# The start of a hybrid encoder on one core: parameter loads on ScalarE's queue, RMS roots on GpSimd, x tile 3 in halves, and other fill-in steps among the mLSTM heads

## The chip, the cores and the metric

The kernel runs on one core of a Trainium2 chip. The metric is the device time of one execution in microseconds; three executions of the kernel before gave 1367.3 to 1371.68, with a median of 1370.09. The engines are TensorE (PE), VectorE (DVE), ScalarE (ACT), GpSimd (POOL) and SyncE (SP), which only issues DMAs here.

## What is computed

One layer of an encoder on x of 512 tokens by 1024 channels, in float32. Cut to what matters:

```python
h = rms_norm(x, norm_mix_g[l])
z = jnp.einsum('bsd,dc->bsc', h, w_in[l])
y_a = jnp.einsum('bsw,wd->bsd', mlstm_branch(z, ...), w_up_a[l])           # 4 heads, both directions
y_b = jnp.einsum('bsw,wd->bsd', diff_attention_branch(z, ...), w_up_b[l])  # 4 heads, ALiBi
g_a = jax.nn.sigmoid(z[..., OFF_GATE:OFF_GATE + D_MODEL])
g_b = jax.nn.sigmoid(z[..., OFF_GATE + D_MODEL:])
x = x + jnp.einsum('bsd,de->bse', g_a * y_a + g_b * y_b, w_out[l])
h2 = rms_norm(x, norm_ffn_g[l])
x = x + expert_choice_ffn(h2, ...)    # 16 experts, 64 tokens each, 1024 -> 2048 -> 1024
return rms_norm(x, norm_f_g)
```

`rms_norm` divides each row of x by the root of its mean square and multiplies by a gain per channel.

## The kernel before

**The trunk** (everything up to the router) works on transposed activations. At the start four tiles of x (`xt`, 128 tokens by 1024 channels) are loaded, squared and summed on ScalarE (L266), turned into reciprocal roots two tiles at a time (`rsqrt_act`: small VectorE steps and a ScalarE square root), and scaled into `xs`. TensorE transposes `xs` into eight PSUM tiles `hps` (L280), first seven of the eight channel blocks of every tile, then the last. ScalarE and VectorE evacuate each of the eight as a high part `hH` and a rest `hL` (`split_evac`, L233 and L234), scaled by the gains in `pc`. The column tile `pc` is the transpose of `prow`, 69 rows of small parameters that six DMAs bring in.

Every projection then takes three matmuls for each block of channels (`zT`: L310 to L312), of weight blocks `raw` that are split likewise into `sp`: the copy on ScalarE (L249), the subtraction on VectorE (L250); for the first block, `pre[0]`, the copy is L283 and the subtraction L284 on GpSimd. `raw` has five buffers. The gate weights `graw`, the gate biases `bi` and `bf`, `lamt` and the router's `wr` come in beside them.

**Order of the work.** Up to `start_order.close()` VectorE and ScalarE run their instructions in the order in which the code is written, and TensorE does so through the whole trunk. GpSimd's and SyncE's instructions are put in order by the framework's scheduler when the kernel is built; on the chip each engine takes its own instructions strictly in the built order. Each DMA that SyncE or ScalarE issues counts on one of eight semaphores, `DMAHW0` to `DMAHW7`, taken in turn, and an issue waits until the last DMA on its semaphore has landed. Each engine's instructions are held up by what waits ahead of them.

**Among the mLSTM heads** TensorE's order is a list of steps. `mlstm_head(h)` yields after each of four score blocks (`sc`, L569 to L571, whose weights VectorE makes at L582), after the first two value products (`pn`, L591) and at the end; VectorE reads `pn` at L599 and so gives its two PSUM buffers back. Between them stand fill-in steps `more`: for heads 0 and 1 the q and k projections of head h + 2, four steps of 12 matmuls; for heads 2 and 3 steps of `gate_b`, the gated up-projection of the attention branch (two half projections, then one step through `w_up_b`).

**The feed-forward part** streams 16 experts' weights through a ring of eleven 2 MB buffers (`mw`), which lie where tiles of the trunk lay. SyncE issues the loads (L995 for gate and up weights, L1163 for down weights) in the order in which they are used.

Of the kernel before, what the change touches and what calls it, by code (L numbers as in the profile page):

```python
# [71 lines left out]
def kernel(  # L72
# [60 lines left out]
    def rsqrt_act(dst, ssq, scale, pool):  # L133
        w = pool.tile([P, 3, 4], F32, tag="rsq", name="rsq", bufs=4)
        v, u = w[:, 0, 0:dst.shape[-1]], w[:, 1, 0:dst.shape[-1]]
        ve.tensor_scalar(v, ssq, scale, EPS, op0=OP.mult, op1=OP.add)
        se.activation(u, v, AF.Sqrt)
        ve.reciprocal(dst, u)
        ve.tensor_mul(u, dst, dst)
        ve.tensor_mul(u, u, v)  # L140
        ve.tensor_scalar(u, u, -0.5, 1.5, op0=OP.mult, op1=OP.add)
        ve.tensor_mul(dst, dst, u)

# [52 lines left out]
    first_sqrt = consts.tile([P, 1], F32, name="first_sqrt")  # L196
    se.activation(first_sqrt, ident[:, 0:1], AF.Sqrt)
# [1 line left out]
    sy.dma_start(prow[0:8], norm_mix_g[0].rearrange("(k p) -> k p", p=P))
    sy.dma_start(prow[8:16], norm_ffn_g[0].rearrange("(k p) -> k p", p=P))  # L200
    sy.dma_start(prow[16:24], conv_b[0].rearrange("(k p) -> k p", p=P))
    sy.dma_start(prow[24:64], conv_w[0].rearrange("w (k p) -> (w k) p", p=P))
    sy.dma_start(prow[64:68], mlstm_norm_g[0].rearrange("(k p) -> k p", p=P))
# [1123 lines left out]
```

## Time and profile before

| | |
|---|---|
| median of 3 executions | 1370.09 us (1367.3 to 1371.68) |
| profiled execution | 1370.63 us, of which its span 1368.3 us |
| busy in the span | PE 95%, DVE 30%, ACT 22%, POOL 10% |
| data moved | 444.02 MB, 325 GB/s over the span |
| first projection matmul (L310) | 16.70 us |
| mLSTM heads | from about 195 to 285 us |
| first weight load of the experts | 390.25 us |

Times inside the profile count from the span's start; the execution's time is longer than the span by what lies before its first and behind its last instruction. The share of busy time is a mean over stages that have different limits: start, trunk, router and expert weights are to be read apart.

### The profile page before, as it was taken

To read this page: it belongs to the slowest core of one execution; us is meant where nothing else is said; L and a number is where in the kernel's file an instruction comes from. 1 tells how busy PE (TensorE), PEld (TensorE's weight loads), DVE (VectorE), ACT (ScalarE), POOL (GpSimd) and SP (SyncE) were. 2 spreads that over 40 slices of the span, in tenths; PEclk is the share of its full clock that TensorE was granted. 3 is DMA by queue.
4 is the path that set the end of the run, shared out by engine and by line. 5 is a ranking of instruction groups with operands and counts; after the bars stand their busy time and mean duration, and the time that the engine had idled before them with its cause. 6 is when DMAs were issued, how large, how long until landed. Compare 5 with 4: busy or idle time off the path is not lost.

```text
span 1368.3 us, 16140 instructions
## 1 busy us (share of the span) xinstructions
PE 1301.3 (95%) x6566; PEld 711.8 (52%) x6566; DVE 415.5 (30%) x982; ACT 304.5 (22%) x621; POOL 131.1 (10%) x239
## 2 busy tenths in 40 slices
PE   8999999999999999999999998999899899889997
PEld 8988897888888534433433432423333242333332
DVE  5687759853443211020030020111102012010241
ACT  7676646433331010100000001000010000001030
POOL 3010212200111011000000000000000000000020
PEclk9999999999999999999999999999999999999999
DMA  7223242223478899999999999999999999999996
GB/s 205 64 64 89 81 109 62 63 77 107 134 280 344 339 425 427 427 428 427 429 428 427 428 427 428 427 428 428 428 427 429 428 427 427 427 428 427 428 427 276
DMA packets 81737, 444.02 MB, mean 325 GB/s; under 512 B 6353, under 2 KB 49431, under 8 KB 54656
## 3 DMA queue, kind: packets, MB, share of 16 engines
q1 hardware_dynamic: 79312, 438.43, 78.6%
q10 hardware_dynamic: 2240, 4.25, 1.3%
q8 instruction: 51, 0.84, 0.2%
q0 software_dynamic: 112, 0.33, 0.1%
q14 instruction: 22, 0.18, 0.0%
HBM read 440.58 MB, written 2.38 MB: 324 GB/s over the span
## 4 chain that ended last, share of the span: by engine, by line
PE 69%; DMA 22%; DVE 4%; issue 3%; ACT 2%; POOL 0%; POOLq 0%; SPq 0%; ACTq 0%; DVEq 0%
DMA w<-in_w_up_e_dram 21%; PE pgate L1083 14%; PE pup L1083 12%; PE pd L1167 7%; PE pg L1034 4%; PE zps L310 4%; PE zps L312 4%; PE zps L311 4%; PE pg L1151 3%; PE pt L1129 1%; PE bank L784 1%; PE bank L786 1%; PE bank L785 1%; PE pa L1053 1%; PE zps L352 1%
## 5 line engine op out<-in xcount | busy, mean ns | idle before, releaser
L1083 PE MATMUL pup<-w,xe 128*64 128x512 f32 x1024 | 240.1, 600 | 27.1 <-DMA w<-in_w_up_e_dram 27.1
L1083 PE MATMUL pgate<-w,xe 128*64 128x512 f32 x1016 | 243.7, 603 | 0.7 <-ACT sh L1272 0.7
L1167 PE MATMUL pd<-w,sh 128*64 128x512 f32 x1024 | 228.5, 597 | 15.4 <-DMA w<-in_w_down_e_dram 13.6
L1167 PEld LDWEIGHTS pd<-w,sh 128*64 128x64 f32 x1024 | 71.2, 137 | 162.6 <-issue 130.8
L1083 PEld LDWEIGHTS pup<-w,xe 128*64 128x64 f32 x1024 | 69.1, 136 | 165.4 <-issue 115.9
L1083 PEld LDWEIGHTS pgate<-w,xe 128*64 128x64 f32 x1016 | 63.0, 136 | 98.5 <-issue 85.2
L1146 DVE SCALAR_TENSOR_TENSOR mats<-pd,ga,mats 64x512 fp32r<-64x512 f32 x30 | 22.5, 750 | 289.1 <-ACT mats L1144 288.6
L310 PE MATMUL zps<-hH,sp 128*128 128x512 f32 x256 | 101.9, 398 | 0.8 <-DVE hL L234 0.8
L312 PE MATMUL zps<-hH,sp 128*128 128x512 f32 x256 | 100.0, 391 | 0.0
L311 PE MATMUL zps<-hL,sp 128*128 128x512 f32 x256 | 99.9, 390 | 0.0
L250 DVE TENSOR_TENSOR sp<-raw,sp 128x512 fp32r<-128x512 f32 x114 | 78.1, 688 | 54.6 <-ACT sp L249 52.0
L1034 PEld LDWEIGHTS pg<-ohr,xn 128*128 128x128 f32 x512 | 64.8, 196 | 45.4 <-issue 44.6
L249 ACT ACTIVATE sp<-raw 128x512 fp32r<-128x512 f32 x114 | 70.9, 630 | 69.5 <-PE zps L620 27.6
L1034 PE MATMUL pg<-ohr,xn 128*128 128x128 f32 x512 | 75.8, 293 | 0.2 <-DVE ohr L1027 0.2
L1284 DVE TENSOR_TENSOR sh<-sh,pup 128x512 f32<-128x512 f32 x32 | 20.6, 684 | 140.2 <-PE pup L1083 133.3
L1144 ACT ACTIVATE mats<-pd,ga 64x512 fp32r<-64x512 f32 x30 | 20.5, 683 | 191.6 <-PE pd L1167 191.3
L1038 ACT ACTIVATE xe<-pg,gff 128x128 f32<-128x128 f32 x32 | 11.8, 368 | 228.8 <-PE pg L1034 228.8
L1133 ACT ACTIVATE sh<-pt 128x512 f32<-128x512 f32 x16 | 9.6, 598 | 237.6 <-PE pt L1129 237.6
L1047 POOL TENSOR_SCALAR mats<-iota,slot 128x64 fp32r<-128x64 f32 x64 | 26.8, 444 | 313.4 <-PE pt L1064 288.2
L310 PEld LDWEIGHTS zps<-hH,sp 128*128 128x128 f32 x256 | 48.1, 188 | 10.6 <-POOL sp L284 1.0
L312 PEld LDWEIGHTS zps<-hH,sp 128*128 128x128 f32 x256 | 48.1, 188 | 10.4
L311 PEld LDWEIGHTS zps<-hL,sp 128*128 128x128 f32 x256 | 48.1, 188 | 9.5
(337 smaller groups left out, 1551.8 us busy)
## 6 DMA issues: line engine op xcount, KB each, us to landing
w<-in_w_down_e_dram SPq DMA_DIRECT2D x59, 2048.0 KB
w<-in_w_gate_e_dram SPq DMA_DIRECT2D x56, 2048.0 KB
w<-in_w_up_e_dram SPq DMA_DIRECT2D x56, 2048.0 KB
raw<-in_w_in_dram SPq DMA_DIRECT2D x44, 512.0 KB
w<-in_w_up_e_dram SPq DMA_DIRECT2D x16, 1024.0 KB
w<-in_w_gate_e_dram SPq DMA_DIRECT2D x15, 1024.0 KB
w<-in_w_down_e_dram SPq DMA_DIRECT2D x8, 1024.0 KB
raw<-in_w_out_dram SPq DMA_DIRECT2D x8, 512.0 KB
```

Source lines behind the costliest of these rows:

```text
L249: se.activation(sp[:, 0], raw, AF.Copy)
L250: ve.tensor_sub(sp[:, 1], raw, sp[:, 0].bitcast(F32))
L310: pe.matmul(zp, w[:, 1], hT(hH, k), start=(k == 0), stop=False)
L311: pe.matmul(zp, w[:, 0], hT(hL, k), start=False, stop=False)
L312: pe.matmul(zp, w[:, 0], hT(hH, k), start=False, stop=(k == ND - 1))
L1034: pe.matmul(pg, xn[t][:, c0:c0 + 255:2], ohr[:, t], start=(t == 0), stop=(t == NT - 1))
L1047: (gp if j else ve).tensor_scalar(oa[:, t, j * CAP:(j + 1) * CAP], iota, slot[:, t, e:e + 1], None, op0=OP.is_equal)
L1083: pe.matmul(pu[s * 64:(s + 1) * 64, c], xe[:, b, half:half + CAP], wt[:, c0:c0 + 512], start=(b == 0), stop=(b == ND - 1))
L1146: ve.scalar_tensor_tensor(yb[r, 1, c], src[r], ga[r, e % 2], yb[r, 0, c].bitcast(F32), op0=OP.mult, op1=OP.subtract)
L1151: pe.matmul(pq, oaT[:, v, t], yb[:, i, cols], start=(i == 0), stop=(i == 1))
L1167: pe.matmul(pd[s * 64:(s + 1) * 64], hid_col(q, i), wt[:, i * D + h * 512:i * D + (h + 1) * 512], start=(c == 0), stop=(c == 15))
L1284: ve.tensor_mul(sg[:, cols], sg[:, cols], pu[:, i])
```

## The change

It has two places.

1. At the start. The six loads into `prow` are issued by ScalarE instead of SyncE, and SyncE issues the first two weight blocks `pre` directly behind x, ahead of `graw`. The first activation function is Exp instead of Sqrt. The roots are taken on GpSimd by a power of -0.5 (`rms`), for tiles 0 and 1 together, tile 2 and tile 3. Tile 3 is squared in two halves, one on ScalarE and one on VectorE, and scaled in two halves. The copies of `pre[0]` on ScalarE now stand ahead of the scaling of tile 3, and the parameters' transpose ahead of x's.
2. Among the heads. For heads 0 and 1 `gate_b` is appended to the list of fill-in steps, and every head gives 2, 2, 1 and 1 steps to its four slots instead of 2, 1, 1 and 2.

```diff
-    first_sqrt = consts.tile([P, 1], F32, name="first_sqrt")
-    se.activation(first_sqrt, ident[:, 0:1], AF.Sqrt)
+    first_exp = consts.tile([P, 1], F32, name="first_exp")
+    se.activation(first_exp, ident[:, 0:1], AF.Exp)
     prow = gt("prow", (NROW, P))
-    sy.dma_start(prow[0:8], norm_mix_g[0].rearrange("(k p) -> k p", p=P))
...
-    sy.dma_start(prow[68:69], diff_norm_g[0:1])
+    se.dma_start(prow[0:8], norm_mix_g[0].rearrange("(k p) -> k p", p=P))
...
+    se.dma_start(prow[68:69], diff_norm_g[0:1])
+    pre = [load_head(c) for c in (DQ, DK)]
     graw = gt("graw", (P, ND, NGATE))
     sy.dma_start(graw, wi[:, MG:MG + NGATE].rearrange("(k p) c -> p k c", p=P))
-    pre = [load_head(c) for c in (DQ, DK)]
...
-    ss = r4.tile([P, 2, NT], F32, name="ss")
-    xs = []
-    for t in range(NT):
...
-        se.activation(xs[t], xt[t], AF.Square, accum_out=ss[:, 0, t:t + 1])
-        if t % 2 == 1:
-            rsqrt_act(ss[:, 1, t - 1:t + 1], ss[:, 0, t - 1:t + 1], 1.0 / D, consts)
-            for i in (t - 1, t):
-                if i == 2:
-                    se.activation(xs[i], xt[i], AF.Copy, scale=ss[:, 1, i:i + 1])
-                else:
-                    ve.tensor_scalar(xs[i], xt[i], ss[:, 1, i:i + 1], None, op0=OP.mult)
+    ss = r4.tile([P, 4, NT], F32, name="ss")
+    gp.memset(ss[:, 3], -0.5)
+
+    def rms(t0, t1):
+
+        v = ss[:, 0, t0:t1]
+        gp.tensor_scalar(v, v, 1.0 / D, EPS, op0=OP.mult, op1=OP.add)
+        gp.tensor_tensor(ss[:, 1, t0:t1], v, ss[:, 3, t0:t1], op=OP.pow)
...
+    for t in range(2):
+        se.activation(xs[t], xt[t], AF.Square, accum_out=ss[:, 0, t:t + 1])
+    rms(0, 2)
+    se.activation(xs[2], xt[2], AF.Square, accum_out=ss[:, 0, 2:3])
+    rms(2, 3)
+    for t in range(2):
+        ve.tensor_scalar(xs[t], xt[t], ss[:, 1, t:t + 1], None, op0=OP.mult)
+        x_T(t, range(ND - 1))
+
+    se.activation(xs[3][:, 0:512], xt[3][:, 0:512], AF.Square, accum_out=ss[:, 0, 3:4])
+    ve.tensor_tensor_reduce(xs[3][:, 512:], xt[3][:, 512:], xt[3][:, 512:], 1.0, 0.0, op0=OP.mult, op1=OP.add,
+                            accum_out=ss[:, 2, 3:4])
+    gp.tensor_add(ss[:, 0, 3:4], ss[:, 0, 3:4], ss[:, 2, 3:4])
+    rms(3, 4)
     sq = [sp_tile((4, P)) for _ in range(2)]
     for i in range(2):
         se.activation(sq[i][:, 0], pre[0][:, 4 * i:4 * i + 4], AF.Copy)
         last_sub = gp.tensor_sub(sq[i][:, 1], pre[0][:, 4 * i:4 * i + 4], sq[i][:, 0].bitcast(F32))
     pre[0] = sq
+    ve.tensor_scalar(xs[2], xt[2], ss[:, 1, 2:3], None, op0=OP.mult)
+    x_T(2, range(ND - 1))
+    ve.tensor_scalar(xs[3][:, 0:512], xt[3][:, 0:512], ss[:, 1, 3:4], None, op0=OP.mult)
+    se.activation(xs[3][:, 512:], xt[3][:, 512:], AF.Copy, scale=ss[:, 1, 3:4])
+    x_T(3, range(ND - 1))
...
-        more = steps(lambda: mlstm_q(h + 2), lambda: mlstm_k(h + 2)) if h < 2 else gate_b
-        for i, (n, m) in enumerate(((2, 2), (2, 1), (1, 1), (1, 2))):
+        more = [gate_b] if h > 1 else [steps(lambda: mlstm_q(h + 2), lambda: mlstm_k(h + 2)), gate_b]
+        for i, (n, m) in enumerate(((2, 2), (2, 2), (1, 1), (1, 1))):
             run(head, n)
             if (h, i) == (0, 1):
                 attn_out(3)
-            run(more, m)
+            for _ in range(m):
+                while next(more[0], 0) == 0:
+                    more.pop(0)
```

How the built programs stand against each other is shown at three places. The names in brackets are the semaphores that an instruction waits for. First ScalarE, at the start of the program. Before, behind the first activation (x tiles 0 to 3 are `x_63`, `x_65`, `x_67` and `x_69`; `raw` is the first weight block):

```order
L266 ACTIVATE xs,ss<-x_63 128x1024 [waits DMAHW1_49]
L266 ACTIVATE xs,ss<-x_65 128x1024 [waits DMAHW2_49]
L137 ACTIVATE rsq<-rsq 128x2 [waits DVE_49]
L266 ACTIVATE xs,ss<-x_67 128x1024 [waits DMAHW3_49]
L266 ACTIVATE xs,ss<-x_69 128x1024 [waits DMAHW4_49]
L137 ACTIVATE rsq<-rsq 128x2 [waits DVE_49]
L271 ACTIVATE xs<-x_67,ss 128x1024 [waits DVE_49,Activation_49]
L283 ACTIVATE sp<-raw 128x512 [waits DMAHW4_49]
L283 ACTIVATE sp<-raw 128x512
```

And now, at the same place:

```order
L188 DMA prow<-in_norm_mix_g_dram 8x128
L189 DMA prow<-in_norm_ffn_g_dram 8x128 [waits DMAHW0_49]
L190 DMA prow<-in_conv_b_dram 8x128 [waits DMAHW2_49]
L191 DMA prow<-in_conv_w_dram 40x128 [waits DMAHW4_49]
L192 DMA prow<-in_mlstm_norm_g_dram 4x128 [waits DMAHW6_49]
L193 DMA prow<-in_diff_norm_g_dram 1x128 [waits DMAHW0_49]
L270 ACTIVATE xs,ss<-x_63 128x1024 [waits DMAHW1_49]
L270 ACTIVATE xs,ss<-x_65 128x1024
L272 ACTIVATE xs,ss<-x_67 128x1024 [waits DMAHW3_49]
L278 ACTIVATE xs,ss<-x_69 128x512
L285 ACTIVATE sp<-raw 128x512 [waits DMAHW5_49]
L285 ACTIVATE sp<-raw 128x512
```

The six loads stand ahead of the Squares, with waits of their own: semaphore 0 is that of `gff` and then of the second `prow` load, semaphores 2 and 4 are those of x tiles 1 and 3, and semaphore 6 is that of the second weight block. The next row of ScalarE is the half scaling of tile 3 (L291, which waits for VectorE and GpSimd), and the eight evacuations stand behind it.

Second GpSimd, behind the memsets at the start of the program. Before:

```order
L284 TENSOR_TENSOR sp<-raw,sp 128x512 [waits DMAHW4_49,Activation_49]
L284 TENSOR_TENSOR sp<-raw,sp 128x512 [waits Activation_49]
L303 TENSOR_SCALAR wr<-wr,pc 128x16 [waits DMASW0_49,DVE_49]
L303 TENSOR_SCALAR wr<-wr,pc 128x16 x7
L450 MEMSET first_305 64x512 [waits Pool_49]
L450 MEMSET first_305 64x512
L470 IOTA first_304 128x896 [waits Pool_49]
```

Now, behind the roots of tiles 0 to 2 (`ss` holds sums and roots; L281 adds the two half sums of tile 3, L257 and L258 are the two steps of `rms`):

```order
L286 TENSOR_TENSOR sp<-raw,sp 128x512 [waits DMAHW5_49,Activation_49]
L286 TENSOR_TENSOR sp<-raw,sp 128x512 [waits Activation_49]
L312 TENSOR_SCALAR wr<-wr,pc 128x16 [waits DMASW0_49,DVE_49]
L312 TENSOR_SCALAR wr<-wr,pc 128x16 x7
L459 MEMSET first_299 64x512 [waits Pool_49]
L459 MEMSET first_299 64x512
L479 IOTA first_298 128x896 [waits Pool_49]
L281 TENSOR_TENSOR ss<-ss 128x1 [waits DVE_49]
L459 MEMSET qk_301 64x512 [waits Pool_49]
L257 TENSOR_SCALAR ss<-ss 128x1 [waits Pool_49]
L459 MEMSET qk_301 64x512
L258 TENSOR_TENSOR ss<-ss 128x1 [waits Pool_49]
```

The root of tile 3 stands behind the subtractions, the router scalings, two memsets and the iota, with two more memsets between its steps.

Third TensorE, at the end of mLSTM head 1: the last rows of the second value products (`pn`), and what stands on either side. Before, the second half of the key projection and then the scores of head 2:

```order
L311 MATMUL zps<-hL_180,sp 128x512
L312 MATMUL zps<-hH_184,sp 128x512
L591 MATMUL pn<-v_1872,first_2388 128x129 x3
L591 MATMUL pn<-v_1872,first_2389 128x129 x2
L591 MATMUL pn<-v_1872,first_2388 128x129 x4
L591 MATMUL pn<-v_1872,first_2389 128x129
L569 MATMUL sc<-mqk 128x512
L570 MATMUL sc<-mqk 128x512
```

Now a step through `w_up_b` stands ahead of them and a half projection of `gate_b` behind:

```order
L628 MATMUL zps<-oL,sp 128x512
L629 MATMUL zps<-oH,sp 128x512
L600 MATMUL pn<-v_1866,first_2419 128x129 x3
L600 MATMUL pn<-v_1866,first_2420 128x129 x2
L600 MATMUL pn<-v_1866,first_2419 128x129 x4
L600 MATMUL pn<-v_1866,first_2420 128x129
L319 MATMUL zps<-hH_183,sp 128x512
L320 MATMUL zps<-hL_179,sp 128x512
```

The key half went ahead of the first value products. Head 0 has a half projection of `gate_b` in each of these two places.

## Rows read from the trace of the kernel before

**Rows 1.** From the page: the span; the data rate in 40 equal slices of the span; the shares of the chain that ended last, by line.

```profile
span 1368.3 us, 16140 instructions
GB/s 205 64 64 89 81 109 62 63 77 107 134 280 344 339 425 427 427 428 427 429 428 427 428 427 428 427 428 428 428 427 429 428 427 427 427 428 427 428 427 276
DMA w<-in_w_up_e_dram 21%; PE pgate L1083 14%; PE pup L1083 12%; PE pd L1167 7%; PE pg L1034 4%; PE zps L310 4%; PE zps L312 4%; PE zps L311 4%; PE pg L1151 3%; PE pt L1129 1%; PE bank L784 1%; PE bank L786 1%; PE bank L785 1%; PE pa L1053 1%; PE zps L352 1%
```

**Rows 2.** What SyncE's queue waited for between 380 and 500 us: line, releaser, us in total, times, longest.

```profile
SPq L995 <- PE bank L786: 28.1, 3, 14.5
SPq L995 <- DVE slot L957: 9.0, 1, 9.0
```

**Rows 3.** Busy us (and instructions) of PE, PEld, DVE, ACT and POOL in four stretches; then the granted TensorE clock, the DMA engines' mean busy share and GB/s.

```profile
380.00:385.00 5.00, 5.00 (x23) 4.06 (x23) 1.99 (x3) 1.86 (x4) 1.21 (x4) 1.00 0.26 94
455.00:460.00 5.00, 5.00 (x27) 2.31 (x26) 0.35 (x1) 0.37 (x1) 0.00 (x0) 1.00 0.70 216
475.00:480.00 5.00, 5.00 (x28) 2.27 (x26) 0.35 (x1) 0.00 (x0) 0.00 (x0) 1.00 1.01 418
20.00:60.00 40.00, 40.00 (x247) 35.95 (x246) 25.45 (x59) 28.66 (x54) 5.26 (x11) 1.00 0.37 107
```

**Rows 4.** SyncE's DMA issues at the start, in order of time: start, us, line, what, count.

```profile
0.80 1.90 SPq L105 DMA_DIRECT2D x<-in_x_dram  x4
2.74 0.63 SPq L199 DMA_DIRECT2D prow<-in_norm_mix_g_dram  x1
...
5.21 0.30 SPq L203 DMA_DIRECT2D prow<-in_mlstm_norm_g_dram  x1
6.12 0.22 SPq L204 DMA_DIRECT2D prow<-in_diff_norm_g_dram  x1
7.76 0.40 SPq L206 DMA_DIRECT2D graw<-in_w_in_dram  x1
9.86 1.02 SPq L183 DMA_DIRECT2D raw<-in_w_in_dram  x2
```

**Rows 5.** ScalarE at the start, in order of time; in brackets the idle time before, and what ended it.

```profile
4.71 1.06 ACT L266 ACTIVATE xs<-x 128x1024 f32<-128x1024 f32 x1 [1.91 <-DMA x<-in_x_dram]
...
7.76 1.06 ACT L266 ACTIVATE xs<-x 128x1024 f32<-128x1024 f32 x1
8.73 0.19 ACT L266 ACTIVATION_READ_ACCUMULATOR xs<-x 128x1 f32 x1
9.86 1.06 ACT L266 ACTIVATE xs<-x 128x1024 f32<-128x1024 f32 x1 [0.94 <-DMA x<-in_x_dram]
...
14.04 1.15 ACT L283 ACTIVATE sp<-raw 128x512 fp32r<-128x512 f32 x2 [0.35 <-DMA raw<-in_w_in_dram]
15.10 4.72 ACT L233 ACTIVATE hH<-hps,pc 128x512 fp32r<-128x512 f32 x8
```

**Rows 6.** Three stretches of the start, columns as in rows 3.

```profile
9.00:10.00 1.00, 1.00 (x12) 1.00 (x11) 1.00 (x2) 0.14 (x1) 0.00 (x0) 1.00 0.64 62
12.00:13.00 1.00, 0.64 (x6) 0.40 (x4) 0.90 (x4) 0.46 (x1) 0.00 (x0) 1.00 1.14 339
13.00:14.00 1.00, 0.25 (x2) 0.26 (x3) 0.60 (x4) 0.69 (x1) 0.00 (x0) 1.00 1.18 316
```

**Rows 7.** GpSimd at the start, in order of time.

```profile
14.77 2.52 POOL L284 TENSOR_TENSOR sp<-raw,sp 128x512 fp32r<-128x512 f32 x2 [11.71 <-ACT sp L283]
17.26 2.48 POOL L303 TENSOR_SCALAR wr<-wr,pc 128x16 f32<-128x16 f32 x8
19.80 1.10 POOL L450 MEMSET first<- 64x512 f32 x2
20.85 0.88 POOL L470 IOTA first<- 128x896 f32 x1
```

**Rows 8.** GpSimd in the router stage: the add, scale and power of one root.

```profile
427.68 0.19 POOL L831 TENSOR_TENSOR lg<-lg 128x1 f32<-128x1 f32 x1 [39.86 <-ACT junk L803]
427.95 0.19 POOL L832 TENSOR_SCALAR lg<-lg 128x1 f32<-128x1 f32 x1
428.23 0.60 POOL L833 TENSOR_TENSOR rst<-lg,mhalf 128x1 f32<-128x1 f32 x1
```

**Rows 9.** TensorE in order of time: the keep-warm matmuls, and the first projection matmul.

```profile
1.79 9.25 PE L168 MATMUL zps<-ident 128*128 128x128 f32 x60 [1.79 <-POOL bf L211]
...
16.70 0.47 PE L310 MATMUL zps<-hH,sp 128*128 128x512 f32 x1 [0.77 <-DVE hL L234]
```

**Rows 10.** A stretch that holds mLSTM head 1, columns as in rows 3.

```profile
220.00:240.00 20.00, 16.80 (x93) 14.08 (x93) 19.03 (x54) 11.39 (x30) 6.84 (x10) 1.00 0.31 79
```

**Rows 11.** TensorE in order of time: the second value products of head 1.

```profile
233.49 2.50 PE L591 MATMUL pn<-v,first 128*128 128x129 f32 x20 [2.75 <-DVE first L599]
```

**Rows 12.** Three stretches of the router stage, columns as in rows 3.

```profile
442.00:444.00 2.00, 1.24 (x6) 1.24 (x7) 1.15 (x5) 0.59 (x4) 0.00 (x0) 0.50 0.98 414
446.00:448.00 2.00, 2.00 (x16) 2.00 (x16) 1.86 (x7) 0.00 (x0) 0.00 (x0) 0.77 0.98 414
448.00:450.00 2.00, 2.00 (x20) 2.00 (x19) 1.83 (x8) 0.00 (x0) 0.00 (x0) 1.00 1.05 442
```

**Rows 13.** TensorE in order of time in that stage.

```profile
442.76 0.42 PE L920 MATMUL tps<-ident,aff 128*64 128x128 f32 x1 [1.29 <-DVE aff L844]
442.98 8.31 PE L168 MATMUL zps<-ident 128*128 128x128 f32 x56
```

More of the change, by code (lines that the diff above doesn't have):

```diff
@@ L131, in rsqrt @@
             ve.scalar_tensor_tensor(dst if i == 2 else y, u, 1.5, y, op0=OP.add, op1=OP.mult)
[L133 to L142, printed above, removed]
     mrow_d = dram.tile([2, H, S], F32, name="mrow_d")
@@ L195 @@
     keep_warm(WARM0)
[L196 to L197 removed]
+    first_exp = consts.tile([P, 1], F32, name="first_exp")
+    se.activation(first_exp, ident[:, 0:1], AF.Exp)
     prow = gt("prow", (NROW, P))
[L199 to L204 removed]
+    se.dma_start(prow[0:8], norm_mix_g[0].rearrange("(k p) -> k p", p=P))
+    se.dma_start(prow[8:16], norm_ffn_g[0].rearrange("(k p) -> k p", p=P))
+    se.dma_start(prow[16:24], conv_b[0].rearrange("(k p) -> k p", p=P))
+    se.dma_start(prow[24:64], conv_w[0].rearrange("w (k p) -> (w k) p", p=P))
+    se.dma_start(prow[64:68], mlstm_norm_g[0].rearrange("(k p) -> k p", p=P))
+    se.dma_start(prow[68:69], diff_norm_g[0:1])
+    pre = [load_head(c) for c in (DQ, DK)]
     graw = gt("graw", (P, ND, NGATE))
     sy.dma_start(graw, wi[:, MG:MG + NGATE].rearrange("(k p) c -> p k c", p=P))
[L207 removed]
     bi = r4.tile([36, 1], F32, name="bi")
@@ L260, in split_head @@
         return [split(raw[:, 4 * i:4 * i + 4], (4, P)) for i in range(2)]
-    ss = r4.tile([P, 2, NT], F32, name="ss")
-    xs = []
-    for t in range(NT):
-        xs.append(st_("xs", (P, D)) if t < 3 else r4.tile([P, D], F32, tag="mqk", name="xs", bufs=2))
-        se.activation(xs[t], xt[t], AF.Square, accum_out=ss[:, 0, t:t + 1])
-        if t % 2 == 1:
-            rsqrt_act(ss[:, 1, t - 1:t + 1], ss[:, 0, t - 1:t + 1], 1.0 / D, consts)
-            for i in (t - 1, t):
-                if i == 2:
-                    se.activation(xs[i], xt[i], AF.Copy, scale=ss[:, 1, i:i + 1])
-                else:
-                    ve.tensor_scalar(xs[i], xt[i], ss[:, 1, i:i + 1], None, op0=OP.mult)
+    ss = r4.tile([P, 4, NT], F32, name="ss")
[4 more added lines that the diff above has]
+        gp.tensor_tensor(ss[:, 1, t0:t1], v, ss[:, 3, t0:t1], op=OP.pow)
+    xs = [st_("xs", (P, D)) if t < 3 else r4.tile([P, D], F32, tag="mqk", name="xs", bufs=2) for t in range(NT)]
     params()
@@ L276, with x_T @@
            for g, n in (("z", 3), ("z", 3), ("z", 3), ("sc", 2), ("sc", 2), ("pv", 2), ("pv", 2), ("tp", 1))]
-    for ks in (range(ND - 1), range(ND - 1, ND)):
-        for t in range(NT):
-            for k in ks:
-                pe.transpose(hps[k][:, t * P:(t + 1) * P], xs[t][:, k * P:(k + 1) * P], ident)
+    def x_T(t, ks):
+        for k in ks:
+            pe.transpose(hps[k][:, t * P:(t + 1) * P], xs[t][:, k * P:(k + 1) * P], ident)
+    for t in range(2):
[11 more added lines that the diff above has]
+    rms(3, 4)
     sq = [sp_tile((4, P)) for _ in range(2)]
@@ L285 @@
     pre[0] = sq
+    ve.tensor_scalar(xs[2], xt[2], ss[:, 1, 2:3], None, op0=OP.mult)
[3 more added lines that the diff above has]
+    x_T(3, range(ND - 1))
+    for t in range(NT):
+        x_T(t, (ND - 1,))
     for k in range(ND):
```

## The prediction

> **What bounds the kernel now.** I read the page's rates first. The data rate is low in the first third and stands at about 428 GB/s from then to the end, and a fifth of the chain that ends last is the expert weights' own DMA [rows 1]: TensorE ends up waiting for that stream. So the end is: the moment when that stream runs without gaps, plus bytes by rate. Next I asked what starts the stream. The weight loads wait on SyncE for matmuls of the output projection and for the routing slots [rows 2], because their buffers lie where the trunk's tiles lay; the DMA engines are a quarter busy just before the first of them, 0.70 busy as late as 455 to 460 us, and full from 475 us [rows 3]. Whatever delays the trunk's TensorE work therefore delays every release, and the end, one for one. Inside the trunk TensorE has no slack to absorb a delay: it is busy in 40.00 of the 40 us after 20 us [rows 3]. What is left to win or lose is the start, before the first projection matmul at 16.70 us [rows 9], and the idle time among the mLSTM heads, 20.00 less 16.80 = 3.2 us [rows 10].
>
> **The start before.** SyncE issues x, then six parameter loads, then the gate columns and the two first weight blocks. Each DMA counts on one of eight semaphores taken in turn, and an issue waits until the semaphore's last user has landed. That is seen: the gate columns go out at 7.76 and the weight blocks at 9.86 us [rows 4], the very moments when ScalarE gets x tiles 2 and 3 [rows 5]. Block 0 is usable at 14.04 [rows 5], 4.18 us after its issue. ScalarE squares each tile as it lands, from 4.71 on, so that x and the block are both ready when the evacuations start at 15.10 [rows 5]; the first projection matmul follows 16.70 - 15.10 = 1.60 us later.
>
> **Part 1, parameter loads on ScalarE.** The built order shows the same waits on their new engine. ScalarE now issues the six parameter loads before its first Square, and they wait in turn for gff, x tile 1, x tile 3 (semaphore 4), the second weight block (semaphore 6) and an earlier parameter load. Behind the fifth stand all four Squares. So the first Square, at 4.71 before, waits until weight block 1 has landed, though it needs x tile 0 alone.
> When does block 1 land? Both blocks, 0.52 MB each, now lie in SyncE's queue directly behind x. x tile 3 lands at 9.86 [rows 5]; blocks of this shape move at 339 and 316 GB/s [rows 6], so 1.05 MB takes 3.2 us: 13.1. I take 12.6, as the small-element gate columns, which hold 0.64 of the DMA engines at 62 GB/s from 9 to 10 us [rows 6], no longer lie beside x's tail. Bounds: 11.5 (x a full 0.8 us earlier, blocks at 427 GB/s) and 14.0 (block 0's own landing before).
> Then two more issues, 0.30 and 0.22 us for these same loads on SyncE [rows 4], and a few hundredths between: first Square at 13.2 to 13.3. A Square with its accumulator read takes 8.73 + 0.19 - 7.76 = 1.16 us [rows 5], three of them 3.5; the half Square of tile 3 about 0.7 (a half-width ScalarE pass took 1.15 / 2 in [rows 5], plus the read): 17.5.
>
> **Part 2, roots on GpSimd.** This takes twelve small VectorE and two ScalarE steps out of the start. One root costs 0.19, 0.19 and 0.60 us for add, scale and power, with starts 0.27 and 0.28 apart [rows 8]: 1.15 us for tile 3, if GpSimd were free. It is not. GpSimd is not ordered by hand here, and in the built order tile 3's add, scale and power stand behind the two subtractions for block 0, the eight router scalings, two fills and an iota, with two more fills between the three. ScalarE's copy of block 0 comes right after the half Square; the first subtraction followed that copy's start by 14.77 - 14.04 = 0.73 us [rows 5, 7], so it starts at 18.2. From there to the iota's end took 20.85 + 0.88 - 14.77 = 6.96 us [rows 7]: 25.2. Add 0.28, fill 0.55, scale 0.28, fill 0.55 [rows 7, 8], power 0.56: 27.4.
> ScalarE waits there for half of tile 3, and its eight evacuations stand behind that wait: 0.6 us for the half, evacuations from 28.0, first projection matmul 1.60 later at 29.6. **Shift: 29.6 - 16.7 = 12.9 us.** The halves themselves save about 0.5 us of this scaling, already counted. The scaling of tiles 0 to 2 and their transposes fit before 27.4.
>
> **Part 3, the clock.** TensorE's keep-warm matmuls still end near 11 us [rows 9], but then it has 21 transposes and long waits until 28. In the router stage, after a wait of 1.29 us and shorter ones, the granted clock stood at 0.50 (1.2 GHz) and came back to full between 446 and 448 us, with matmuls running without a gap since 442.98; 6, 16 and 20 matmul records fall into stretches of 2 us there [rows 12, 13]. I expect the eleven last transposes and the first few projection groups at half speed. Between nothing and 2.6 us I take 1.4, since the evacuations pace that projection anyway.
>
> **Part 4, the rest of the start.** The weight blocks go out 7 us earlier; this gains nothing while tile 3's root is the later input. One activation-table load disappears behind the first projection; TensorE never waited there [rows 3], and were that cover gone it would return about a microsecond. Later loads keep their place behind the bias loads on SyncE and find TensorE later than before.
>
> **Part 5, fill-in among the heads.** For heads 0 and 1 the last slot had nothing to run. Now the second key half moves ahead of the first value products, and steps of the branch-b projection stand after them and after the second. The work is only moved. The most it can win is the 3.2 us of idle, nearly all of it a wait of 2.75 us of value products for VectorE in head 1 [rows 11]. But VectorE is busy 19.03 of 20 us there [rows 10], so it is the backlog that counts: two more TensorE steps of 12 matmuls come ahead of that wait, and each brings VectorE only one or two splits. It should catch up by most of the 2.75 us. I take 2.0; bounds 3.2, and a loss of 1.0 if the convolution of the key, which now ends just ahead of the value products, leaves the same wait in two places.
>
> **Sum.** The profiled execution took 1370.63 us, of which its span is 1368.3; the median of the three runs is 1370.09, so the sum reads the same against either. 1370.6 + 12.9 + 1.4 - 2.0 = **1382.9 us**.
>
> **A rule against this change.** The rows show that the time an issue holds its engine is not the 0.2 to 0.6 us of the issue but the wait ahead of it: SyncE stood from 6.34 to 7.76 and 8.16 to 9.86 [rows 4]. The Trainium skill, "DMA: Bandwidth & Descriptors", section "Issuing engines are not separate DMA queues", says that issuing from several engines saves only the sequencer time of the issue; section "Anatomy of one DMA — SWDGE (gpsimd) path" of that page adds that any semaphore wait happens on the issuing sequencer. Its first rule alone would give rival B below, its second the sum above; the trace agrees with the second.
>
> **The rivals.** A, the weight stream hides the late start: a late trunk would cost nothing if the first weight loads were released by something else than the trunk, and the time would be 1370.6, or 1368.6 with the heads' gain: no change. It decides if SyncE's weight loads still go out near 390 us. Against it: they waited for trunk matmuls [rows 2]. Chance 0.03.
> B, ScalarE pays only the issue time: six issues of 0.22 to 0.63 us, first Square near 5. Then block 0 (landed at about 11.4) and GpSimd's queue set the start: subtraction at 12.1, iota's end 19.1, power 21.3, first matmul 23.5, a shift of 6.8, with clock and heads 1370.6 + 6.8 + 1.4 - 2.0 = 1376.8. Against it: the named semaphores. Chance 0.05.
> C, neither holds: tile 3 lands at 9.86, its root is ready 0.73 + 1.15 later, blocks are copied meanwhile, evacuations start near 13.2, first matmul 14.8: 1.9 gained, with the heads' 2.0 to 3.2 the time is 1365.5 to 1366.7. It would take a GpSimd that passes its queue. Chance 0.03.
> D, dearer than the sum: block 1 at 14.0, the clock's whole 2.6, a head lost: 1370.6 + 14.3 + 2.6 + 1.0 = 1388.5, or beyond if the slow clock lasts through the first key projection. Chance 0.06.
>
> **How the numbers follow.** The forecast has 0.83. Its own bounds are 1370.6 + 11.8 + 0 - 3.2 = 1379.2 and about 1387. The range takes in B's side and stops short of D: 1376.5 to 1388. A difference under 0.3%, 4.1 us, can't be told from none here. C gives faster 0.02 and a little of no change; with A, no change 0.04; all else is slower, 0.94.
>
> **What would show it.** In the changed profile: ScalarE's first Square at 13 us or later, waiting for a DMA, with x tile 0 long there; GpSimd's power for tile 3 after the iota, at 26 to 28.5; first projection matmul at 28 to 31; SyncE's first weight load moved from 390.25 to about 402; idle among the heads under 1.5 us. A first Square before 10 us breaks part 1; a power before 22 us breaks part 2; a weight load that still starts near 390 breaks the one-for-one rule and with it the whole forecast.

## The result, and the profile after

| | before | after |
|---|---|---|
| median | 1370.05 us (1367.3 to 1371.68) | 1384.48 us (1383.94 to 1387.41, 4 executions) |
| profiled execution, and its span | 1370.63, 1368.3 | 1383.94, 1382.2 |
| first Square of ScalarE | 4.71 | 14.31 |
| first projection matmul | 16.70 | 32.46 |
| first scores of head 0 | 195.2 | 211.7 |
| first output-projection matmul | 385.1 | 400.1 |
| first weight load of the experts | 390.25 | 405.26 |
| first matmul of the experts (`pg`) | 453.8 | 468.2 |

The ratio is 1.0105, with a 95% interval of 1.009 to 1.0119: slower by 14.4 us. The forecast of 1382.9 was 1.6 us short, and its range of 1376.5 to 1388.0 holds the time.

The page of the changed kernel answers to [rows 1]. The DMA share of the chain that ended last is 20% (21 before); the rate reaches its plateau of about 427 GB/s one to two slices of the span later.

```profile
span 1382.2 us, 16129 instructions
GB/s 157 93 77 62 60 109 77 74 79 79 135 180 371 336 416 421 426 430 425 429 427 429 426 429 426 429 426 429 427 429 426 430 426 427 428 428 427 428 426 288
DMA w<-in_w_up_e_dram 20%; PE pgate L1094 14%; PE pup L1094 12%; PE pd L1178 7%; PE pg L1045 4%; PE zps L319 4%; PE zps L321 4%; PE zps L320 4%; PE pg L1162 3%; PE pt L1140 1%; PE bank L795 1%; PE bank L797 1%; PE bank L796 1%; PE pa L1064 1%; PE zps L361 1%
```

SyncE's first loads of expert weights in order of time, and what its queue waited for between 395 and 515 us: line, releaser, us in total, times, longest. The releasers are those of [rows 2], trunk matmuls and the routing slots; the first load goes out 15.0 us later.

```profile
405.26 0.61 SPq L1006 DMA_DIRECT2D w<-in_w_gate_e_dram  x1
...
SPq L1006 <- PE bank L797: 28.0, 3, 14.5
...
SPq L1006 <- DVE slot L968: 9.0, 1, 9.0
```

ScalarE's start in order of time, to be read beside [rows 5]. L191 and L192 are the fourth and the fifth parameter load, L270 the first Square, L278 the half Square of tile 3, L285 the copy of block 0, L291 the half scaling of tile 3, L222 the evacuations.

```profile
9.95 0.29 ACTq L191 DMA_DIRECT2D prow<-in_conv_w_dram  x1
13.70 0.26 ACTq L192 DMA_DIRECT2D prow<-in_mlstm_norm_g_dram  x1
...
14.31 1.06 ACT L270 ACTIVATE xs<-x 128x1024 f32<-128x1024 f32 x1 [11.51 <-DMA prow<-in_mlstm_norm_g_dram]
...
17.44 0.61 ACT L278 ACTIVATE xs<-x 128x512 f32<-128x512 f32 x1
...
18.05 1.13 ACT L285 ACTIVATE sp<-raw 128x512 fp32r<-128x512 f32 x2
29.05 0.72 ACT L291 ACTIVATE xs<-x,ss 128x512 f32<-128x512 f32 x1 [9.86 <-POOL ss L258]
30.71 3.58 ACT L222 ACTIVATE hH<-hps,pc 128x512 fp32r<-128x512 f32 x6 [0.94 <-PE hps L267]
```

ScalarE does nothing for 11.51 us before its first Square. In [rows 5] x tile 0 let that Square start at 4.71, so some 9.6 us of this belong to the parameter loads. It does nothing again for 9.86 us, until GpSimd's power (L258) is done. GpSimd in order of time, beside [rows 7]: L257 and L258 for the first tiles, the subtractions L286, the router scalings L312, fills and iota (L459, L479), and between them tile 3's add (L281), scale and power.

```profile
17.68 0.75 POOL L257 TENSOR_SCALAR ss<-ss 128x1 f32<-128x1 f32 x1
18.52 0.94 POOL L258 TENSOR_TENSOR ss<-ss 128x1 f32<-128x1 f32 x1
19.43 3.01 POOL L286 TENSOR_TENSOR sp<-raw,sp 128x512 fp32r<-128x512 f32 x2
22.44 2.45 POOL L312 TENSOR_SCALAR wr<-wr,pc 128x16 f32<-128x16 f32 x8
24.94 1.09 POOL L459 MEMSET first<- 64x512 f32 x2
26.00 0.88 POOL L479 IOTA first<- 128x896 f32 x1
26.86 0.18 POOL L281 TENSOR_TENSOR ss<-ss 128x1 f32<-128x1 f32 x1
...
28.45 0.56 POOL L258 TENSOR_TENSOR ss<-ss 128x1 f32<-128x1 f32 x1
```

TensorE's last transposes and the first projection matmul, which [rows 9] has at 16.70:

```profile
30.20 2.61 PE L267 MATMUL hps<-ident,xs 128*128 128x128 f32 x11 [7.01 <-DVE xs L290]
32.46 0.77 PE L319 MATMUL zps<-hH,sp 128*128 128x512 f32 x1
```

And stretches of the start, columns as in [rows 3], so that the last three numbers are the granted clock, the DMA engines' share and GB/s. The clock is 0.50 of full speed, 1.2 GHz, while the last transposes run, after TensorE had waited 7.01 us, and 1.00 from 34 us. The DMA engines have nothing to do at 28 to 34 us: SyncE's next block waits for a split on VectorE (L239), which stands behind the evacuations.

```profile
28.00:32.00 4.00, 1.80 (x9) 1.80 (x10) 1.66 (x2) 2.01 (x4) 2.17 (x4) 0.50 0.00 0
32.00:34.00 2.00, 2.00 (x8) 1.73 (x7) 2.00 (x4) 2.00 (x4) 0.00 (x0) 0.59 0.00 0
34.00:36.00 2.00, 2.00 (x10) 1.66 (x9) 2.00 (x4) 2.00 (x5) 0.00 (x0) 1.00 0.03 8
```

What TensorE waited for from 180 to 320 us, first in the kernel before, then in the changed one: line, releaser, us in total, times, longest. The rows of `pn` are the value products among the heads: 3.6 us before, with the long wait of [rows 11], and 2.7 now.

```profile
PE pn L591 <- DVE first L599: 3.0, 2, 2.7
PE pn L591 <- DVE rsq L129: 0.6, 2, 0.5
```

```profile
PE pn L600 <- DVE first L608: 2.7, 3, 1.4
PE zps L361 <- DVE sp L239: 1.7, 1, 1.7
```

The last row lies ahead of the heads' scores, and the kernel before has such a wait of 1.4 us there.

### The profile page after: what moved, and what is told of

It reads as the page before. It is cut to its first block, busy times and chain, and to the rows that moved or that the text cites. A ratio compares the mean times of both kernels' runs of the same rounds, so it can differ in the third digit from the quotient of the medians.

```text
span 1382.2 us, 16129 instructions
## 1 busy us (share of the span) xinstructions
PE 1302.9 (94%) x6566; PEld 714.6 (52%) x6566; DVE 419.2 (30%) x973; ACT 300.9 (22%) x618; POOL 136.9 (10%) x247
## 4 chain that ended last, share of the span: by engine, by line
PE 69%; DMA 21%; DVE 4%; issue 3%; ACT 2%; POOL 1%; SPq 0%; POOLq 0%; ACTq 0%; DVEq 0%
DMA w<-in_w_up_e_dram 20%; PE pgate L1094 14%; PE pup L1094 12%; PE pd L1178 7%; PE pg L1045 4%; PE zps L319 4%; PE zps L321 4%; PE zps L320 4%; PE pg L1162 3%; PE pt L1140 1%; PE bank L795 1%; PE bank L797 1%; PE bank L796 1%; PE pa L1064 1%; PE zps L361 1%
## 5 line engine op out<-in xcount | busy, mean ns | idle before, releaser
L1094 PE MATMUL pup<-w,xe 128*64 128x512 f32 x1024 | 241.6, 603 | 28.5 <-DMA w<-in_w_up_e_dram 28.5
L1178 PE MATMUL pd<-w,sh 128*64 128x512 f32 x1024 | 227.2, 594 | 14.3 <-DMA w<-in_w_down_e_dram 12.7
L239 DVE TENSOR_TENSOR sp<-raw,sp 128x512 fp32r<-128x512 f32 x114 | 79.3, 700 | 53.4 <-ACT sp L238 50.8
L1155 ACT ACTIVATE mats<-pd,ga 64x512 fp32r<-64x512 f32 x30 | 20.5, 682 | 189.9 <-PE pd L1178 189.6
```

Source lines behind the costliest of these rows:

```text
L239: ve.tensor_sub(sp[:, 1], raw, sp[:, 0].bitcast(F32))
L1094: pe.matmul(pu[s * 64:(s + 1) * 64, c], xe[:, b, half:half + CAP], wt[:, c0:c0 + 512], start=(b == 0), stop=(b == ND - 1))
L1178: pe.matmul(pd[s * 64:(s + 1) * 64], hid_col(q, i), wt[:, i * D + h * 512:i * D + (h + 1) * 512], start=(c == 0), stop=(c == 15))
```

## The experiments

The questions were these. Are the two queues, ScalarE's and GpSimd's, each worth what the sum gave them? Is it block 1's landing that held ScalarE? What do the clock and the fill-in cost or give? The kernel before ran beside each group of experiments, with medians of 1370.58 (e1 to e4), 1370.86 (e5 to e8) and 1370.70 us (e9 to e11). Times are medians, for e9 and e10 that of one execution; the middle columns are read from the trace of one execution each.

| | first Square | tile 3's root there | first projection matmul | head 0's scores | output projection | from scores to output projection | time |
|---|---|---|---|---|---|---|---|
| before | 4.71 | 12.44 | 16.70 | 195.2 | 385.1 | 189.9 | 1370.05 |
| after | 14.31 | 29.01 | 32.46 | 211.7 | 400.1 | 188.4 | 1384.48 |
| e1, new start, old fill-in | 13.97 | 28.64 | 32.09 | 211.7 | 403.6 | 191.9 | 1387.55 |
| e2, old start, new fill-in | 4.64 | 12.30 | 16.50 | 195.1 | 383.6 | 188.5 | 1367.78 |
| e3, parameters on SyncE | 4.64 | 23.21 | 25.77 | 205.2 | 393.5 | 188.3 | 1377.26 |
| e4, GpSimd in order | 14.20 | 21.17 | 24.73 | 203.8 | 392.2 | 188.4 | 1376.48 |
| e5, e3 and e4 | 4.58 | 18.75 | 22.32 | 201.1 | 389.5 | 188.4 | 1374.09 |
| e6, three queues mended | 4.76 | 12.13 | 15.67 | 194.3 | 382.7 | 188.4 | 1368.27 |
| e7, TensorE kept busy | 14.25 | 29.92 | 32.49 | 211.2 | 399.5 | 188.3 | 1384.86 |
| e8, one block ahead | 12.52 | 27.21 | 30.65 | 209.8 | 398.1 | 188.3 | 1382.11 |
| e9, kernel before again | 4.52 | 11.75 | 15.87 | 194.2 | 385.6 | 191.4 | 1370.45 |
| e10, e1 again | 14.08 | 28.79 | 32.23 | 211.5 | 401.4 | 189.9 | 1385.43 |
| e11, e5 with the old fill-in | 4.53 | 18.48 | 22.05 | 200.6 | 392.5 | 191.9 | 1377.39 |

**e1 and e2: one place of the change at a time.** e1 has the new start with the old list of fill-in steps, e2 the old start with the new list:

```diff
-        more = steps(lambda: mlstm_q(h + 2), lambda: mlstm_k(h + 2)) if h < 2 else gate_b
+        more = [gate_b] if h > 1 else [steps(lambda: mlstm_q(h + 2), lambda: mlstm_k(h + 2)), gate_b]
```

Expected of e1: 

> The changed start, with the fill-in of the kernel before among the heads. My theory, after the changed kernel's profile: the start alone costs 15 to 16 us at the first projection matmul (32.5 against 16.7 us) and the new fill-in wins back only about 1 us, so this kernel takes about 1385.3 us, 1.011 of before, with the first projection matmul at 32.5 and 3.5 us of TensorE idle among the heads. Rival: the fill-in wins 2 us as forecast; then 1386.5. Other rival: the fill-in wins nothing; then 1384.5.

Expected of e2: 

> The start of before, with the new fill-in among the heads. My theory: TensorE idle among the heads falls from 3.6 us to about 2.7, the time by about 1 us to 1369.1, 0.9993 of before. Rival, the forecast: 2 us less, 1368. Other rival: nothing or a loss, 1370 or more.

Measured: e1 1387.55 us, ratio 1.0132 (1.0116 to 1.0147); e2 1367.78 us, ratio 0.9981 (0.9972 to 0.999). The start alone costs 17.0 us, the fill-in alone gives 2.8, or 3.1 between e1 and the changed kernel. So e1 lies above all three times expected of it, and e2 falls to that of the forecast and not to mine of about 1 us. TensorE in e2, in order of time: the wait of 2.75 us did not go. It was divided among heads 0 and 1, two waits of 1.07 and 1.37 us and a short one, 2.64 in all.

```profile
214.65 1.38 PE L591 MATMUL pn<-v,first 128*128 128x129 f32 x10 [0.20 <-DVE first L599]
217.11 1.38 PE L591 MATMUL pn<-v,first 128*128 128x129 f32 x10 [1.07 <-DVE first L599]
241.36 2.50 PE L591 MATMUL pn<-v,first 128*128 128x129 f32 x20 [1.37 <-DVE first L599]
```

From the first scores to the output projection e2 is 1.4 us shorter than the kernel before, and e1 3.5 longer than the changed kernel. That difference is taken up by e9 to e11.

**e3: parameters on SyncE.** The six loads are issued by SyncE again, behind `pre` and ahead of `graw`; everything else is as in the changed kernel.

```diff
-    se.dma_start(prow[0:8], norm_mix_g[0].rearrange("(k p) -> k p", p=P))
...
     pre = [load_head(c) for c in (DQ, DK)]
+    sy.dma_start(prow[0:8], norm_mix_g[0].rearrange("(k p) -> k p", p=P))
...
```

Expected: 

> The changed kernel, but the six parameter loads are issued by SyncE, behind the two weight blocks. This takes ScalarE's hold away and leaves the scheduler its order of GpSimd, where tile 3's root now stands behind even the router scalings and four fills. My theory (the two causes stand in series): first Square at 4.7 us, block 0 at about 12.5, GpSimd's queue from 13.2 to 22.4, power at 23.5, first projection matmul near 26, time about 1378.5. Rival (ScalarE's hold is the whole loss): first projection matmul before 18, time 1371 or less.

Measured: 1377.26 us, ratio 1.0055 (1.0039 to 1.007). ScalarE's first Square, and then tile 3's add and power on GpSimd, behind the second iota:

```profile
4.64 1.06 ACT L270 ACTIVATE xs<-x 128x1024 f32<-128x1024 f32 x1 [1.84 <-DMA x<-in_x_dram]
```

```profile
21.20 0.87 POOL L479 IOTA first<- 128x896 f32 x1
22.02 0.10 POOL L762 MEMSET tk<- 128x2 f32 x1
22.08 0.19 POOL L281 TENSOR_TENSOR ss<-ss 128x1 f32<-128x1 f32 x1
...
22.64 0.57 POOL L258 TENSOR_TENSOR ss<-ss 128x1 f32<-128x1 f32 x1
```

The Squares are 9.7 us earlier, the first projection matmul only 6.7: GpSimd's queue still holds the root until its second iota is done. The two queues in series were expected to give 26 us there, ScalarE's hold alone less than 18.

**e4: GpSimd in order.** `start_order` also orders GpSimd by the code, in which the root stands ahead of the subtractions.

```diff
-    start_order.enter_context(tc.manual_schedule(engines={mybir.EngineType.DVE, mybir.EngineType.Activation}))
+    start_order.enter_context(tc.manual_schedule(engines={mybir.EngineType.DVE, mybir.EngineType.Activation,
+                                                          mybir.EngineType.Pool}))
```

Expected: 

> The changed kernel, but GpSimd too runs the start in the written order, so that tile 3's root stands ahead of the subtractions, scalings and fills; ScalarE keeps its hold. My theory (in series): first Square at 14.3 as in the changed kernel, VectorE's half sum at 19.7, power at 20.9, first projection matmul near 24, time about 1376.5. Rival (GpSimd's queue costs nothing, since the hold sets the start): first projection matmul at 32, time 1384.

Measured: 1376.48 us, ratio 1.0045 (1.003 to 1.006). GpSimd's rows for tile 3 in order of time, and after them the subtractions:

```profile
19.70 0.56 POOL L282 TENSOR_TENSOR ss<-ss 128x1 f32<-128x1 f32 x1 [0.35 <-DVE ss L280]
20.35 0.19 POOL L258 TENSOR_SCALAR ss<-ss 128x1 f32<-128x1 f32 x1
20.62 0.55 POOL L259 TENSOR_TENSOR ss<-ss 128x1 f32<-128x1 f32 x1
21.14 2.69 POOL L287 TENSOR_TENSOR sp<-raw,sp 128x512 fp32r<-128x512 f32 x2
```

The root is there at 21.17 instead of 29.01, with ScalarE's first Square left at 14.20. Mending either queue alone takes away about half of the shift, 7.2 and 8.0 us of time, which is what a series of the two gives.

**e5: both.** Expected: 

> The changed kernel with both of the edits that were tried alone: the six parameter loads issued by SyncE behind the first two weight blocks, and GpSimd ordered by hand in the start, so that tile 3's root stands ahead of the subtractions. If the two queues are all that makes the start late, the two savings (7.2 and 8.0 us) add up: about 1369.3 us, first projection matmul near 17. If a third queue takes over, it is VectorE's: the copy of the parameter columns stands there ahead of all scaling of x, and it ran at 14.92 us with the loads on SyncE; from that copy to the first projection matmul took 24.73 - 15.84 = 8.9 us in the kernel with GpSimd ordered, less the 1.2 us in which VectorE waited there for the root of tiles 0 and 1: first projection matmul at 22.6, time about 1374.

Measured: 1374.09 us, ratio 1.0022 (1.0012 to 1.0032), first projection matmul at 22.32. Against the changed kernel that is 10.4 us, not the 15.2 of both savings; a third queue takes over, as the second case expected of it had (22.6 and 1374). VectorE in order of time: its first instruction of the start is the copy of the parameter columns, behind which all scaling of x stands, and the parameters land late because SyncE issues them behind the blocks.

```profile
14.71 0.23 DVE L234 COPY pc<-tps 128x69 f32<-128x69 f32 x1 [14.71 <-PE tps L233]
...
15.12 1.41 DVE L276 TENSOR_SCALAR xs<-x,ss 128x1024 f32<-128x1024 f32 x2
```

The roots of tiles 0 and 1 had been there at 8.25 us. This is the change's third move, to which the forecast gave nothing: in the changed kernel it is covered by the other two. What moved is VectorE's copy. TensorE took the parameters' transpose ahead of x's before too, at 10.88 us, but VectorE took the copy at 13.15, behind its scaling of x.

**e6: all three mended.** On top of e5, the parameter loads stand ahead of the blocks on SyncE, `params()` behind the scaling of x, and ScalarE's half of tile 3 ahead of its copies of block 0:

```diff
-    params()
...
+    se.activation(xs[3][:, 512:], xt[3][:, 512:], AF.Copy, scale=ss[:, 1, 3:4])
     sq = [sp_tile((4, P)) for _ in range(2)]
...
     x_T(3, range(ND - 1))
+    params()
```

Expected: 

> As the kernel before with regard to the queues, and with what the change has to offer otherwise: the parameter loads on SyncE ahead of the two weight blocks and the blocks ahead of the gate columns; GpSimd ordered by hand, root ahead of subtractions; ScalarE's half of tile 3 ahead of its copies of block 0; the parameters' transpose and copy behind the scaling of x; the new fill-in among the heads. If the three queues were all that was wrong with the new start, x tile 3 lands at 9.8, its root is there at 11.9, its halves at 12.6 to 13.4, evacuations start near 13.9 and the first projection matmul at 15.5: 1.0 before that of the kernel with the new fill-in alone (1367.8), so 1366.8 us, faster than both kernels. Rival: small GpSimd steps run slow beside VectorE's scaling (0.75 and 0.94 us instead of 0.19 and 0.56), the root comes 1.5 us later and nothing is gained over the VectorE roots: 1368.3.

Measured: 1368.27 us, ratio 0.9982 (0.9973 to 0.9991): faster than both kernels, if only by 0.2% against the kernel before, and by this comparison no different from e2, whose ratio was 0.9981. The time is the rival's, 1368.3, but its mechanism was not seen: tile 3's root came at 12.13 (expected 11.9) and the first projection matmul at 15.67 (15.5). That is 0.83 before e2's, but e9 shows the unchanged start with 15.87, so single starts differ by as much. Roots on GpSimd, halves and early blocks thus cost nothing that can be seen once no queue is in their way, and no gain from them is shown. What each of e6's three further moves gives by itself was not tried.

**e7: TensorE kept busy.** 50 instead of 30 matmuls at the start, 12 more behind the parameters, 34 more ahead of tile 3's transposes.

Expected: 

> The changed kernel with TensorE kept busy in its waits of the start: 50 instead of 30 matmuls at the start, 12 behind the parameters' transpose, 34 ahead of the transposes of tile 3; nothing else moves. If the half clock costs what the shift of the first projection (15.8 us) has over the forecast's chain, its transposes and the first projection matmuls run at full clock, the first projection matmul comes near 31.2 instead of 32.5 and the time falls by 1.3 to 2: about 1382.8. Rival: the evacuations on ScalarE pace that stretch, the clock costs nothing: 1384.5.

Measured: 1384.86 us, ratio 1.0098 (1.0082 to 1.0114): no gain in time. The rows show why. TensorE in order of time, and a stretch:

```profile
22.15 7.76 PE L271 MATMUL hps<-ident 128*128 128x128 f32 x68
30.50 1.42 PE L267 MATMUL hps<-ident,xs 128*128 128x128 f32 x11 [0.60 <-DVE xs L295]
32.49 0.47 PE L325 MATMUL zps<-hH,sp 128*128 128x512 f32 x1 [0.57 <-DVE hL L223]
```

```profile
30.00:32.00 2.00, 1.42 (x11) 1.19 (x11) 0.85 (x2) 1.81 (x3) 0.00 (x0) 1.00 0.00 0
```

The clock stayed at 1.00, and the eleven transposes took 1.42 us instead of 2.61. But GpSimd's fills now stand in another order, and the root of tile 3 came at 29.92 instead of 29.01. Counted from the root, the first projection matmul came after 2.57 us instead of 3.45, and head 0's scores after 181.2 instead of 182.7, 1.5 us less. Not all of this is the clock. VectorE's half scaling of tile 3 had to be done before the transposes. Here it is in the changed kernel, with GpSimd's row beside it, then in e7 and in e3, where GpSimd had nothing to do behind the root:

```profile
28.98 0.88 POOL L479 IOTA first<- 128x896 f32 x1
29.05 1.09 DVE L290 TENSOR_SCALAR xs<-x,ss 128x512 f32<-128x512 f32 x1 [7.72 <-POOL ss L258]
```

```profile
29.96 0.49 DVE L295 TENSOR_SCALAR xs<-x,ss 128x512 f32<-128x512 f32 x1 [8.69 <-POOL ss L258]
```

```profile
23.25 0.49 DVE L290 TENSOR_SCALAR xs<-x,ss 128x512 f32<-128x512 f32 x1 [3.98 <-POOL ss L258]
```

So the transposes began 0.58 us after the root in e7 and 1.19 in the changed kernel; these 0.6 us are GpSimd's iota beside VectorE. Counted from the first of these transposes, head 0's scores came after 180.7 us instead of 181.5. The slow clock thus cost about 0.9 us in the changed kernel, most of it behind the first projection matmul; as a saving in time this was not shown. e3 agrees: its first projection matmul came 2.56 us after the root, as soon as e7's, though its clock read 0.50 from 25 to 27 us.

**e8: one block ahead.** The second block is loaded behind the gate biases; the loads of the parameters stay on ScalarE.

```diff
-    pre = [load_head(c) for c in (DQ, DK)]
+    pre = [load_head(DQ)]
...
-    pre += [load_head(c) for c in (DQ + P, DK + P)]
+    pre += [load_head(c) for c in (DK, DQ + P, DK + P)]
```

Expected: 

> The changed kernel with only the first weight block (not the second) ahead of the parameter loads; the second is loaded behind the gate biases. No parameter load then shares a semaphore with the second block: the waits left on ScalarE are for gff, x tiles 1 and 3, a bias load and earlier parameter loads. If the second block's landing is what held ScalarE, the first Square comes about 1.2 us after x tile 3 lands at 9.9, at 11.1 instead of 14.31, and the first projection matmul 3.2 earlier, near 29.3: about 1381.2 us. If ScalarE is held by its place behind the issues as such, whatever they wait for, the first Square stays near 14 and the time at 1384.5.

Measured: 1382.11 us, ratio 1.0079 (1.0064 to 1.0095). ScalarE in order of time:

```profile
11.53 0.29 ACTq L191 DMA_DIRECT2D prow<-in_conv_w_dram  x1
...
12.52 1.06 ACT L270 ACTIVATE xs<-x 128x1024 f32<-128x1024 f32 x1 [9.72 <-DMA prow<-in_mlstm_norm_g_dram]
```

The first Square came 1.79 us earlier, the first projection matmul 1.81, the output projection 2.0. So the second block did hold ScalarE, and the start is paid one for one. It came 1.4 us later than expected of it, since the fourth parameter load went out only at 11.53, where I had counted on x tile 3 as the last wait. In the built order the next semaphore in turn is that of a bias load; that this load's landing was the wait is inferred from there.

**e9 to e11: the same wait with and without the clock.** e9 is the kernel before, e10 is e1, each once more; e11 is e5 with the old fill-in.

Expected of e9: 

> The kernel before once more, for a second look at its wait of 2.75 us in mLSTM head 1. In its first profile the granted clock stayed at 1.00 behind that wait; in the changed start with the old fill-in it stood at 0.50 for some 6 us behind a wait of 2.72 us. If the clock's fall hangs on where in time the wait comes, and not on the wait alone, this profile reads 1.00 again if the start has the same times, and the first output-projection matmul comes 189.9 us after the first scores of head 0. If it falls now and then by chance, it may read 0.50 here, and that distance 192.

Expected of e10: 

> The changed start with the old fill-in once more. If the fall of the clock in head 1 belongs to this kernel, the clock reads 0.50 again near 250 to 256 us and the distance from the first scores to the first output-projection matmul is 191.9 us again; if it comes by chance, it may read 1.00 and the distance 189.9.

Expected of e11: 

> The kernel with both edits of the start (parameter loads on SyncE behind the blocks, GpSimd ordered by hand), now with the old fill-in, so that the wait of 2.7 us in head 1 comes some 5.9 us later than in the kernel before. Against the same start with the new fill-in (1374.1 us): if the fill-in is worth the 1.5 us that the traces show between the first scores and the output projection, 1375.6; if the wait also costs the clock here, as in the kernel with the changed start alone, 3.1 to 3.5 more: 1377.4.

Measured: 1370.45, 1385.43 and, with ratio 1.0049 (1.0032 to 1.0065), 1377.39 us. Each has the wait, of 2.76, 2.76 and 2.74 us; in e1 it was 2.72. Stretches right behind it, first of e1, then of e9, e10 and e11:

```profile
250.00:252.00 2.00, 2.00 (x9) 2.00 (x10) 1.21 (x6) 1.50 (x3) 1.27 (x1) 0.50 0.00 0
```

```profile
234.00:236.00 2.00, 2.00 (x12) 2.00 (x10) 1.58 (x4) 0.69 (x2) 0.23 (x1) 0.50 0.00 0
```

```profile
250.00:252.00 2.00, 2.00 (x19) 2.00 (x19) 1.21 (x6) 1.92 (x5) 1.27 (x1) 1.00 0.00 0
252.00:254.00 2.00, 2.00 (x11) 1.65 (x11) 2.00 (x7) 1.82 (x6) 0.00 (x0) 1.00 0.03 6
```

```profile
240.00:242.00 2.00, 2.00 (x11) 2.00 (x11) 0.91 (x2) 0.94 (x3) 0.66 (x1) 0.50 0.00 0
242.00:244.00 2.00, 2.00 (x10) 1.90 (x9) 1.61 (x5) 0.91 (x4) 0.00 (x0) 0.50 0.01 3
```

The clock fell in e9, where it had stayed full in the first profile of the same kernel [rows 10]; it stayed full in e10, where it had fallen in e1. So one kernel with one wait has both outcomes. With the old fill-in the way from the first scores to the output projection took 189.9 us in the two profiles in which the clock stayed, and 191.4 to 191.9 in the three in which it fell; with the new one it took 188.3 to 188.5 in all eight. With the clock up the new fill-in is thus worth 1.5 us: on that way TensorE is idle for 2.7 us instead of 3.65, and its matmuls, the same in number, are busy for some 0.5 us less. It is worth 1.5 to 2.0 more in each execution in which the long wait would have lowered the clock; e11's time is the one expected of it for that case. What decides that in one execution stays open.

## Why the prediction was right, point by point

**One for one: right.** Against the kernel before, the changed one is late by 15.8 us at the first projection matmul, 16.5 at the scores, 15.0 at the output projection and at the first weight load, 14.4 at the experts' first matmul, and 13.9 in the span. Rival A is out.

**Part 1: right, its term a little small.** The first Square came at 14.31 (forecast 13.2 to 13.3), because the issue that waited for block 1 went out at 13.70 and not at 12.6, near the upper bound of 14.0. Half of this is the guess that without the gate columns beside it x's tail would land sooner: x tile 3 released its semaphore at 9.95, as before. The other half is the blocks themselves: from there it took 3.75 us and not 3.2, at 289 GB/s from 10 to 12 us, where [rows 6] had 316 to 339. Rival B needed a Square near 5 us; e3 shows that this is what SyncE's queue gives, and ScalarE's does not. The Trainium skill, "DMA: Bandwidth & Descriptors", section "Issuing engines are not separate DMA queues", counts only the time of the issue as what another engine saves. Here the six issues took 0.26 to 0.55 us each and their engine stood for 11.51, some 9.6 more than before.

**Part 2: right, with two costs left out.** Power started at 28.45 (forecast sign 26 to 28.5) and its end came 1.6 us later than the sum's 27.4. Of this, 1.1 is the later Square, and 1.1 lies in GpSimd's queue: the first subtraction came 1.38 us after the copy (0.73 in [rows 5, 7]), since GpSimd was still at the roots of the other tiles, and the two subtractions took 3.01 us (2.52) beside VectorE's passes. Faster Squares, a step of 1.05 us instead of 1.16, and a shorter half Square gave 0.5 back. From the power's end to the first projection matmul it took 3.45 us where the sum had 2.2. The sum lets the evacuations start when ScalarE's half is scaled, 0.6 us after the root, and puts the transposes in between at nothing. They started 1.70 us after it: VectorE's half was done only after 1.1 us, and ScalarE then stood 0.94 us for the transposes.

**Part 3: right in kind, too large.** Against the 1.4 us chosen between 0 and 2.6, e7 gives about 0.9. The clock did fall for the last transposes and the first projection groups, as forecast.

**Part 4: right here, for the reason given.** What was costed at nothing lay behind tile 3's root. Of VectorE's copy of the parameter columns ahead of its scaling of x, which the forecast did not cost, e5 shows what it costs once the cover is gone, together with the place of the parameters on SyncE: e6 takes both back, and its first projection matmul is 6.65 us earlier.

**Part 5: right in sign and size, wrong in its picture.** The waits among the heads fell only from 3.6 to 2.7 us, not under 1.5: part of the long wait moved to head 0. The trace gives 1.5 us (taken: 2.0), the medians 2.8 (e2), 3.1 (e1) and 3.3 (e11), which fits executions with the clock down, of which one profile of the kernel before showed nothing. That this is the whole difference is not shown. The mean granted clock on record points that way: of the 42 executions of the kernel before beside the experiments the 16 with a mean under 0.994 took 1371.6 us on average, the other 26 took 1370.2.

**The error of 1.6 us** in the time is made of a shift and clock 2.2 us larger in the trace (16.5 at the scores, against 14.3), and a rest that cancels part of it. That the time came so close is in part luck: the chain up to the first projection matmul, without the clock, was about 2.6 us too short, the clock 0.5 too dear, and the fill-in gave more in the medians than the 2.0 taken.

## What to carry to other kernels

A DMA issue on a compute engine costs that engine every wait that stands ahead of the issue, so read the waits in the built order before moving loads there. When the start has several queues in series, mending one shows the next: here ScalarE's issues, GpSimd's fills, and VectorE's first copy together with SyncE's order had to move before the new start was no worse than the old one. A wait of TensorE can cost more than its length, and one profile may not show it: compare several executions before pricing such a wait.
